# Two Fourier inputs as a ninth block group, three gate groups' first products moved to the conditioning stage, and a norm by token halves

## The chip, the cores and the metric

The kernel runs on one core of a Trainium2 chip. The metric is the device time of one execution in microseconds. Before the change three runs gave 1305.84, 1305.91 and 1307.22 us, with a median of 1305.91. A further execution was recorded by the hardware profiler, and every line of profile in this document is read from such a recording. The engines are called PE (the matrix engine, TensorE), ACT (ScalarE), DVE (VectorE), POOL (GpSimd) and SP (SyncE); all but DVE issue DMA transfers here.

## The reference

One layer of a backbone block on 512 tokens of width 2048 (`D`), with 256 context tokens; all data are float32. Cut to what matters here:

```python
shift, scale, gate = jnp.split(silu_c @ w_ada[l] + b_ada[l], 3, axis=-1)
h = _modulate(_rmsnorm(xs, norm_g[l]), shift[:, None], scale[:, None])   # xn * (1 + scale) + shift
...
p = h @ w_l                                   # 2048 -> 9216 columns: q, k, v, z_a, u_b, z_b, g_a, g_b
attn = _attention(q, concat([k, kc]), concat([v, vc]))
...
g_a, g_b = jax.nn.sigmoid(p[..., GA]), jax.nn.sigmoid(p[..., GB])
y_a = (attn * jax.nn.silu(z_a)) @ w_pa
y_b = (_fourier_mix(u_b) * jax.nn.silu(z_b)) @ w_pb   # real part of a 2-D FFT over 512 tokens x 128 channels, 4 channel groups
y = (g_a * y_a + g_b * y_b) @ w_o
new_xs = xs + gate[:, None] * y               # then a last rmsnorm
```

## The kernel before

Every product of float32 values is made of three matmuls in a reduced format (`mm3`, L326): each operand is split into a high part (`split_from`, ACT at L177) and a low part (DVE at L178), and high times high, high times low and low times high are added in PSUM. So "a product" of a 128 x 128 block with 512 columns is three matmuls of the form 128x512. Weights arrive by DMA as pieces of 128 x 1024 values, 512 KB each, which a list of requests (`stream`, `get`) loads ahead and splits in turn.

The work runs in stages, one after another on PE.

**Conditioning stage** (L453 to L657). x is loaded transposed in chunks (`XCH`, L106, L465). `token_norms` (L480) squares it on ACT and DVE, sums over the width with eight float32 matmuls (L497), takes roots (L501) and a reciprocal (L502), and `spread` (L505) lays the result over all partitions. Then comes a loop over the 16 blocks `kb` of 128 features. `modulation(kb)` (L584) is a matvec of silu(c) with 2 MB of modulation weights, sixteen 32x256 matmuls (L534) on weights that lie in four buffers of 1 MB (`wada_load`, L460, by POOL's queue from kb 3 on). `columns` (L539) copies its result out (ACT, L542), turns it by two transposes (L545) and adds up four rows (DVE, L551), which gives shift and gain of this kb. Two PSUM buffers (`bank2`) take turns in it. `make_h` (L519) scales x (DVE, L521), and makes the high half (ACT, L522) and the low half (DVE, L523) of h. For kb from 8 on, `form_row` (L601) makes two of the sums of blocks that the groups need later. Between these, PE multiplies by columns that need only the h made so far: `start_work` (L559) computes u and z of the Fourier branch, 8 column tiles of 128 x 16 kb x 3 matmuls, in the order of `STEPS`. Here the weights are the stationary operand and the 512 tokens the moving one, so the sums lie channel by token. Half of them stay in PSUM; the others are added up in SBUF by DVE (L564).

**Fourier stage** (L661 to L728). `channels` multiplies u by a cosine and sine table over the 128 channels, `positions` by a table over the tokens, each time with 256 moving columns, 144 matmuls in all. `gate_b` multiplies by silu(z). The result goes to DRAM (`b_d`) and comes back during attention.

**Eight groups** of 1024 columns of the input projection (`KINDS`, L65): three with q and z_a, two with g_a, one with k and v, two with g_b. A group is a product of h (512 x 2048) by 2048 x 1024 weights cut into 2 x 2 blocks, computed with seven block products instead of eight (Strassen's method in Winograd's form). `PRODUCTS` (L55) names for each product the form of h, what weights it takes, and its accumulator; P1, Q5, P2, Q6, P7, Q3 and Q4 run in the order `ONE_GROUP` (L57). One block product is 8 blocks of k x 2 tiles of 128 tokens x 3 matmuls = 48 matmuls 128x512. Accumulator "a" lies in the PSUM tile x, "b" in y and "c" in x again. When a product ends, ACT or DVE takes the sum out (`steps`, L862 to L902): P1's is copied to `self.X` and Q5's to `self.Y`, by ACT; the others are combined by DVE and handed to `done`, which for a gate group applies a sigmoid and stores the result (`gate_done`). P2 goes on adding to P1's accumulator. Combined weights are made in four buffers `R` by DMAs that add (L281, POOL's queue); P2, P7 and Q3 take plain loads.

**After that** follow attention, with products of the other branch filled in between (`filler`, which first reads `b_d`), two groups for the branch projections (10, 11) and two for the output projection. The output group 8 runs in the order `OUT_GROUP` (L58), in which P1 and P2 stand side by side.

Most orders come from the program's text and from due times: `issue_after` puts an instruction behind another, a list of small jobs is called once per piece, and each engine executes its instructions in the order in which they stand. PE, ACT and DVE therefore wait in line: what stands behind a waiting instruction waits too.

## Time and profile before

| | before |
|---|---|
| median of three runs | 1305.91 us |
| profiled execution, its own time | 1305.55 us |
| span in the profile | 1303.3 us |
| PE, DVE, ACT busy | 1279.5, 995.1, 685.4 us |
| first product of the conditioning stage | 23.47 us |
| Fourier matmuls | 148.75 to 169.39 us |
| eight groups | 169.39 to 808.0 us |
| moved by DMA | 318.54 MB, mean 244 GB/s |

The span runs from the first to the last recorded instruction; the execution's own time has 2.25 us around it. Busy times are sums over instructions. PE's matmuls overlap, so the duration of a single one is longer than the distance to the next. A group shows as one line and operation with "out<-in" by the tiles' names (buffer numbers left out), and in brackets behind a row stands the engine's idle time just before it and whose result ended it. DMA share is the busy share of 16 DMA engines.

### The profile page before, as it was taken

The numbers are of one execution on the slowest core, as the hardware profiler recorded it, in microseconds if no ns is written. First come the engines' busy times: TensorE is split into PE (matmuls) and PEld (weight loads), VectorE is DVE, ScalarE is ACT, GpSimd is POOL, SyncE is SP. The second block draws the span as 40 slices with busy tenths as digits, with TensorE's granted clock in tenths as the row PEclk, the third lists the DMA queues.
The fourth block names the chain that finished last, engine by engine and source line by source line (L and its number), as shares of the span: only waits on it lengthen the run. The fifth ranks groups of instructions, "written<-read, shape, count | busy, mean of one in ns | idle before, by whom it ended". The sixth has DMA issues, their size and how long they took to land.

```text
span 1303.3 us, 17544 instructions
## 1 busy us (share of the span) xinstructions
PE 1279.5 (98%) x6522; PEld 1047.4 (80%) x6522; DVE 995.1 (76%) x1295; ACT 685.4 (53%) x1079; POOL 180.6 (14%) x244
## 2 busy tenths in 40 slices
PE   6999999999999999999999999999999999999997
PEld 3577888888888888888888888888888888888885
DVE  4666899979688887657687766688798867887676
ACT  5222655555556465444254554666666646464544
POOL 0110011110202111011021010011110212221210
PEclk9999999999999999999999999999999999999999
DMA  9898487887899988976879897468872899998985
GB/s 382 338 373 349 178 244 183 242 243 255 209 284 260 265 287 271 292 209 179 273 200 267 294 224 258 169 221 245 251 230 82 236 246 250 244 212 232 220 205 173
DMA packets 103718, 318.54 MB, mean 244 GB/s; under 512 B 9808, under 2 KB 33104, under 8 KB 99280
## 3 DMA queue, kind: packets, MB, share of 16 engines
q0 software_dynamic: 30288, 123.75, 40.4%
q1 hardware_dynamic: 48720, 163.65, 35.3%
q10 hardware_dynamic: 24624, 30.02, 6.6%
q8 instruction: 51, 0.84, 0.2%
q14 instruction: 35, 0.29, 0.1%
HBM read 283.30 MB, written 34.09 MB: 244 GB/s over the span
## 4 chain that ended last, share of the span: by engine, by line
PE 91%; DMA 3%; DVE 2%; ACT 2%; issue 1%; SPq 0%; ACTq 0%; DVEq 0%
PE banks L328 10%; PE banks L329 10%; PE banks L330 10%; PE x L328 9%; PE x L330 9%; PE x L329 9%; PE y L329 7%; PE y L328 7%; PE y L330 7%; PE pd L534 2%; PE banks L1294 2%; PE pb L328 2%; PE pb L330 2%; PE pb L329 2%; DMA wa<-in_w_ss 1%; PE pc L328 1%
## 5 line engine op out<-in xcount | busy, mean ns | idle before, releaser
L177 ACT ACTIVATE whi<-R 128x1024 fp32r<-128x1024 f32 x138 | 145.2, 1059 | 140.2 <-PE banks L330 47.3
L178 DVE TENSOR_TENSOR wlo<-R,whi 128x1024 fp32r<-128x1024 f32 x138 | 167.5, 1221 | 55.4 <-ACT whi L177 55.2
L178 DVE TENSOR_TENSOR wlo<-wr,whi 128x1024 fp32r<-128x1024 f32 (+1 forms) x123 | 148.5, 1212 | 63.4 <-ACT whi L177 63.2
L177 ACT ACTIVATE whi<-wr 128x1024 fp32r<-128x1024 f32 (+1 forms) x123 | 128.8, 1051 | 116.6 <-PE y L330 37.4
L328 PE MATMUL banks<-whi,s 128*128 128x512 f32 x396 | 157.1, 397 | 2.2 <-DVE ev L862 1.5
L330 PE MATMUL banks<-whi,s 128*128 128x512 f32 x396 | 155.2, 392 | 0.0
L329 PE MATMUL banks<-wlo,s 128*128 128x512 f32 x396 | 155.1, 392 | 0.0
L328 PE MATMUL x<-whi,s 128*128 128x512 f32 x352 | 137.2, 390 | 0.0
L330 PE MATMUL x<-whi,s 128*128 128x512 f32 x352 | 137.0, 389 | 0.0
L329 PE MATMUL x<-wlo,s 128*128 128x512 f32 x352 | 137.0, 389 | 0.0
L328 PE MATMUL y<-whi,s 128*128 128x512 f32 x316 | 123.1, 389 | 0.4 <-DVE cxe L1015 0.4
L329 PE MATMUL y<-wlo,s 128*128 128x512 f32 x316 | 123.1, 390 | 0.3 <-DVE wlo L178 0.3
L330 PE MATMUL y<-whi,s 128*128 128x512 f32 x316 | 122.8, 389 | 0.0
L281 POOL DMA_DIRECT2D R<-in_w_g x64 | 55.9, 874 | 420.2 <-DVE wlo L178 247.5
L177 ACT ACTIVATE s<-wr 128x512 fp32r<-128x512 f32 (+2 forms) x93 | 60.4, 676 | 68.6 <-DMA wr<-cf_d 21.8
L178 DVE TENSOR_TENSOR s<-wr,s 128x512 fp32r<-128x512 f32 (+2 forms) x93 | 66.8, 749 | 31.7 <-ACT s L177 30.9
L328 PEld LDWEIGHTS banks<-whi,s 128*128 128x128 f32 x396 | 74.4, 188 | 17.7 <-ACT whi L177 1.9
L330 PEld LDWEIGHTS banks<-whi,s 128*128 128x128 f32 x396 | 74.4, 188 | 15.5
L329 PEld LDWEIGHTS banks<-wlo,s 128*128 128x128 f32 x396 | 74.4, 188 | 14.0 <-DVE wlo L178 0.2
L330 PEld LDWEIGHTS x<-whi,s 128*128 128x128 f32 x352 | 66.1, 188 | 13.8
L329 PEld LDWEIGHTS x<-wlo,s 128*128 128x128 f32 x352 | 66.1, 188 | 13.6
L328 PEld LDWEIGHTS x<-whi,s 128*128 128x128 f32 x352 | 66.1, 188 | 13.6
(293 smaller groups left out, 2829.4 us busy)
## 6 DMA issues: line engine op xcount, KB each, us to landing
wr<-in_w_g SPq DMA_DIRECT2D x128, 512.0 KB, 5.2
R<-in_w_g POOLq DMA_DIRECT2D x64, 512.0 KB, 7.5
wa<-in_w_ss POOLq DMA_DIRECT2D x26, 1024.0 KB, 8.2
R<-in_w_g SPq DMA_DIRECT2D x32, 512.0 KB, 5.6
wr<-in_w_gate SPq DMA_DIRECT2D x32, 512.0 KB, 5.1
wr<-in_w_o SPq DMA_DIRECT2D x24, 512.0 KB, 7.7
R<-in_w_o POOLq DMA_DIRECT2D x24, 512.0 KB, 9.5
wr<-in_w_pab SPq DMA_DIRECT2D x20, 512.0 KB, 6.4
```

The lines of the kernel that those rows point to most:

```text
L177: first = nc.scalar.activation(hi, src, ACT.Copy)
L178: return first, nc.vector.tensor_tensor(lo, src, hi.bitcast(F32), op=ALU.subtract)
L281: nc.gpsimd.dma_start(chain[e.pc], e.nxt, accum_op=ALU.add)
L328: nc.tensor.matmul(o, ah, bh, start=start, stop=False, skip_group_check=cont)
L329: nc.tensor.matmul(o, ah, bl, start=False, stop=False, skip_group_check=cont)
L330: nc.tensor.matmul(o, al, bh, start=False, stop=stop, skip_group_check=cont)
L534: last = nc.tensor.matmul(acc[32 * j : 32 * j + 32, :256], c2[:, 8 * h + k, :], w[:, k, :], start=n < 4, stop=n >= KK - 4)
L1294: nc.tensor.transpose(tp[:, k * P : (k + 1) * P], p[:, k * P : (k + 1) * P], ident)
```

## The change

1. u and z become a ninth group of 1024 columns (`U`, kind "uz"), the first in `ORDER`, with the seven block products in the order `OUT_GROUP`. Their sums are stored to DRAM (`uz_d`). The forms of h that group 0 made during its products (`between`) are made in U.
2. The conditioning stage multiplies instead by the first 512 columns of groups 3, 6 and 7 (`EARLY`), all 16 blocks of k: 3 x 2 token tiles x 16 x 3 = 288 matmuls, which are P1 and P2 of these groups. h is now the stationary operand. The three sums stay in PSUM (`sums_e`). The sum over the first 8 blocks is P1: after kb 7 it is copied and stored (`x1_kept`, `x1_d`). After kb 15 the whole sum gets its sigmoid and is stored (`gate_kept`). Groups 3, 6 and 7 then run five products (`EARLY_GROUP`, `early_end`) and load P1's sum as `X`.
3. x lies as [half of tokens, feature block, 256]. Only the first 256 tokens are normed at the start (`norm_first`), and `make_h` works on them alone for kb below 8. The second half is loaded on POOL's queue (`X_MORE`), squared in kb 6 and 7, normed after kb 7 (`norm_second`), and used from kb 8 on; `form_row` scales the second half of the earlier blocks.
4. The matvecs and norms use two halves of one PSUM tile (`two_d`) in turn.
5. The Fourier stage goes behind the last group. u's sums and differences, and the splits of the tables, are jobs in the last group; `positions` comes first (48 matmuls 128x512), then `channels` (24 matmuls 128x512, and 16 transposes of z). Nothing goes through `b_d`.
6. The pieces of context work spread over 20 pieces of group 3 and 28 of group 4.

```diff
+U = -1
+EARLY = (3, 6, 7)
+EARLY_PIECES = ([((0, 0),), ((0, 1), (0, 2)), ((1, 0), (1, 1)), ((1, 2),)]
+                + [p for k in range(2, KK, 2) for p in (((k, 0), (k, 1)), ((k, 2), (k + 1, 2)), ((k + 1, 0), (k + 1, 1)))])
+EARLY_GROUP = ("Q3", "Q5", "Q6", "P7", "Q4")
+ORDER = (U, *range(len(KINDS)))
+X_MORE = {3: (0,), 4: (4,), 5: (8,), 6: (12,)}
+def products_of(g):
+    return EARLY_GROUP if g in EARLY else OUT_GROUP if g == U else ONE_GROUP
...
+    sums_e = [psp.tile([P, 2, 512], F32, tag=t, bufs=n, name=uid("pb")) for t, n in (("x", 2), ("x", 2), ("y0", 1))]
+    two_d = psp.tile([P, 2, 512], F32, tag="y1", bufs=1, name="pd")
+    def bank2():
+        turn_d[0] ^= 1
+        return two_d[:, turn_d[0], :]
+    def load_x(h, a, n, q=None):
+        (q or nc.sync).dma_start(xt[:, h, a : a + n, :], xT[h, :, a : a + n, :])
     for a, n in XCH:
-        nc.sync.dma_start(xt[:, a : a + n, :], xT[:, a : a + n, :])
+        load_x(0, a, n)
...
+    def square_more(i):
+        if i % 4 == 0:
+            squares.append(new_ev())
+        t = squares[-1][:, 0, :]
+        q = 2 * i
+        a, b = (t[:, :256], t[:, 256:]) if i % 4 == 0 else (squares[-1][:, 1, :256], squares[-1][:, 1, 256:])
+        for o, k in ((a, q), (b, q + 1)):
+            nc.scalar.activation(o, xt[:, 1, k, :], ACT.Square)
+        if i % 4:
+            nc.vector.tensor_tensor(t, t, squares[-1][:, 1, :], op=ALU.add)
+    def norm_second():
+        acc = bank2()
+        n = 0
+        for s in squares:
+            for k in range(2):
+                nc.tensor.matmul(acc[:, :256], ones, s[:, 0, 256 * k : 256 * k + 256], start=n == 0, stop=n == 3)
+                n += 1
+        norm_root(1, acc[:, :256])
+        nc.scalar.copy(rx[:, 1, :], spread(1, acc[:, 256:]))
...
+    def normed(kb, hs, rr):
+        v = xt[:, hs, kb, :]
+        return nc.vector.scalar_tensor_tensor(v, v, gain[:, kb, 0:1], rr, op0=ALU.mult, op1=ALU.mult)
+    def x1_kept(i, a):
+        t = new_ev()
+        nc.scalar.copy(t, a)
+        nc.scalar.dma_start(x1_d[i], t.rearrange("p t c -> p (t c)"))
+    def early_work():
+        for n, (_, what) in enumerate(early_pieces()):
+            wh, wl = get(("early", n))
+            for m, (kb, i) in enumerate(what):
+                a = sums_e[i]
+                for t in range(2):
+                    c = slice(P * t, P * t + P)
+                    mm3(a[:, t, :], hhi[kb][:, c], hlo[kb][:, c], wh[:, m, :], wl[:, m, :], kb == 0, kb in (7, KK - 1),
+                        cont=kb >= 8)
+                if kb == 7:
+                    x1_kept(i, a)
+                elif kb == KK - 1:
+                    gate_kept(EARLY[i], 0, 0, a, None)
+                yield kb
...
+        if kb in X_MORE:
+            for a in X_MORE[kb]:
+                load_x(1, a, 4, nc.gpsimd)
+        if kb in (6, 7):
+            for i in range(4 * (kb - 6), 4 * (kb - 6) + 4):
+                square_more(i)
+        if kb == 7:
+            norm_second()
...
+        def early_end(self, name, a):
+            if name == "Q3":
+                self.V = self.new()
+                nc.scalar.copy(self.V, a)
+            elif name == "Q5":
+                self.Y = self.new()
+                nc.scalar.copy(self.Y, a)
+            elif name == "Q6":
+                sub(self.X, a, self.X)
+                sub(self.V, self.X, self.V)
+                sub(self.Y, self.X, self.Y)
+                self.done(0, 1, self.X, self.X)
+            elif name == "P7":
+                sub(self.V, self.V, a)
+                self.done(1, 1, self.V, self.V)
+            elif name == "Q4":
...
+    def fourier():
+        def positions(g):
+            acc, c = pair("x"), slice(P * g, P * g + P)
+            for e in range(2):
+                for r in range(2):
+                    mm3(acc[:, e, :], uf[e][0][:, r, c], uf[e][1][:, r, c], fs[e][0][:, r, :], fs[e][1][:, r, :],
+                        r == 0, r == 1)
+                split_from(acc[:, e, :].rearrange("p (c n) -> p c n", c=2), hi[:, :, e, :], lo[:, :, e, :])
+        def channels(g):
...
+                nc.tensor.transpose(zt[:, t * P : t * P + P], z[t // 2][:, k : k + P], ident)
...
+                mm3(acc, fc[0][:, 0, s], fc[0][:, 1, s], hi[:, c, :], lo[:, c, :], c == 0, c == 1)
...
+        positions(0)
+        positions(1)
+        channels(0)
+        positions(2)
+        channels(1)
+        positions(3)
+        channels(2)
+        channels(3)
...
-    for g, kind in enumerate(KINDS):
+    for g in ORDER:
+        kind = "uz" if g == U else KINDS[g]
+        if g in EARLY:
+            group.X = new_ev()
+            nc.gpsimd.dma_start(flat(group.X), x1_d[EARLY.index(g)])
+            elif (g, name) == (LAST, "Q6"):
+                jobs += [lambda: None, u_forms]
+    fourier()
```

## The prediction

> **What bounds the kernel now.** I read the page first: the busy shares, the slices, the chain that ended last; then PE's waits, then windows cut where the stages change.

> ```profile
> span 1303.3 us, 17544 instructions
> PE 1279.5 (98%) x6522; PEld 1047.4 (80%) x6522; DVE 995.1 (76%) x1295; ACT 685.4 (53%) x1079; POOL 180.6 (14%) x244
> PE   6999999999999999999999999999999999999997
> PE 91%; DMA 3%; DVE 2%; ACT 2%; issue 1%; SPq 0%; ACTq 0%; DVEq 0%
> ...
> PE pd L497 <- DVE s L496: 8.5, 1, 8.5
> PE banks L328 <- DVE ev L862: 1.5, 1, 1.5
> ...
> 0.00:24.00 24.00, 13.85 (x66) 7.01 (x67) 12.17 (x28) 15.52 (x27) 1.90 (x11) 1.00 0.93 370
> 24.00:42.00 18.00, 17.53 (x117) 9.98 (x115) 7.76 (x16) 4.35 (x9) 2.34 (x4) 1.00 1.01 417
> 42.00:148.75 106.75, 106.61 (x766) 74.75 (x765) 73.42 (x143) 35.86 (x53) 11.83 (x22) 1.00 0.82 313
> 148.75:169.39 20.64, 20.38 (x158) 19.57 (x156) 20.04 (x29) 11.29 (x19) 0.54 (x1) 1.00 0.61 226
> 169.39:245.90 76.51, 76.51 (x340) 63.37 (x339) 73.68 (x86) 43.36 (x64) 9.97 (x12) 1.00 0.82 223
> 655.00:731.50 76.50, 76.50 (x339) 63.38 (x338) 56.73 (x64) 38.01 (x67) 12.29 (x13) 1.00 0.87 261
> 731.50:808.00 76.50, 76.50 (x341) 63.34 (x340) 50.97 (x54) 38.28 (x46) 9.67 (x14) 1.00 0.82 229
> ```

> TensorE bounds it: 1279.5 of 1303.3 us busy, so all its idle time is 23.8 us, 8.5 of it one wait at the start. Seven columns follow each window: length, then busy time of PE, PEld, DVE, ACT and POOL, granted clock, DMA share, GB/s. From 42 us on PE is full. The first two windows show what else is near its limit: 417 GB/s at a DMA share of 1.01. A group of seven products is 76.50 us, all PE; in the first one DVE is busy 73.68 of it. With PE that full, the change can win only the PE work it removes, and loses every us in which its new order leaves PE waiting.

> **Prices.** Three timelines of PE, its neighbours beside it (start, duration, engine, line):

> ```profile
> 88.55 1.93 PE L534 MATMUL pd<-wa,c 128*32 128x256 f32 x32
> 90.42 0.50 PE L328 MATMUL pc<-s,whi 128*128 128x512 f32 x1
> 90.61 0.37 ACT L542 COPY ado<-pd 128x256 f32<-128x256 f32 x1 [5.81 <-PE pd L534]
> 91.22 0.38 PE L545 MATMUL pd<-ident,ado 128*128 128x128 f32 x2
> 91.36 0.47 PE L328 MATMUL pc<-s,whi 128*128 128x512 f32 x1
> 91.71 0.17 DVE L551 TENSOR_REDUCE adr<-pd 128x4 f32<-128x16 f32 x1 [2.36 <-PE pd L545]
> 92.38 0.75 DVE L521 SCALAR_TENSOR_TENSOR xt<-xt,gain,rx 128x512 f32<-128x512 f32 x1
> 93.16 0.72 ACT L522 ACTIVATE s<-xt,shift 128x512 fp32r<-128x512 f32 x1 [2.18 <-DVE xt L521]
> 93.29 0.40 PE L330 MATMUL pc<-s,wlo 128*128 128x512 f32 x1
> 93.62 1.93 PE L534 MATMUL pd<-wa,c 128*32 128x256 f32 x32
> 93.64 0.47 DVE L608 SCALAR_TENSOR_TENSOR Z<-xt,d 128x256 f32<-128x256 f32 x1
> ...
> 147.62 0.39 PE L329 MATMUL pc<-s,whi 128*128 128x512 f32 x1
> 147.84 0.39 PE L330 MATMUL pc<-s,wlo 128*128 128x512 f32 x1
> ...
> 160.03 0.28 PE L328 MATMUL pb<-fsq,ah 128*128 128x256 f32 x1
> 160.15 0.28 PE L329 MATMUL pb<-fsq,ah 128*128 128x256 f32 x1
> ```

> Dense matmuls start 0.2275 us apart at 512 columns (147.62, 147.84) and 0.12 at 256 (160.03, 160.15), less than the shown durations, since they overlap. The kb chain is: matvec ends about 90.42, its columns turn from 91.22 (0.80 later), and the high half of h is there at 93.16 + 0.72 = 93.88: 3.46 us after the matvec. At 256 columns xt costs about 0.47 (L608) for 0.75, and hi about 0.37 (the 256-wide copy) for 0.72: 2.83.

> **The PE work itself.** Removed: 384 products of u and z (128x512) and the 144 Fourier matmuls at 256. Added: 3 groups x 16 k x 2 columns x 3 = 288 in the conditioning stage; nine groups with 6 x 336 + 3 x 240 = 2736 instead of 8 x 336 = 2688; the late Fourier with 48 + 24 and 16 transposes. In 512-wide matmuls +24, in 256-wide -144: 5.5 - 17.3 + 2 for the transposes = -10 us. If PE stayed dense that would be the result. It does not, for the reasons below.

> **Start of the conditioning stage.** The first early product waits for the first norm, now on 256 columns, yet the built program puts the four second-half x loads on POOL's queue without a wait, ahead of the modulation weights of kb 3, so both halves share the saturated engines (1.01) from the start. I take 22 us. The trace of before starts its first product at:

> ```profile
> 23.47 0.73 PE L328 MATMUL pb<-s,whi 128*128 128x512 f32 x2 [0.30 <-ACT s L522]
> ```

> [...]

> **A pair of kb.** In the built program's PE order, a pair below kb 8 reads: 18 products of kb, 7 matvec matmuls, transposes, 9 of the next matvec, 12 products, 7 matvecs, 3 products, transposes, 3 products, 9 matvecs, 18 products. Before, nine products of older k stood behind the transposes (91.36 to 93.29); now products that need this very kb's hi stand there. Between the matvec's end and them lie, in the even case, the transposes (0.2) and nine of sixteen matvec matmuls (9/16 of the 1.87 from 88.55 to 90.42: 1.05); in the odd case six products (1.4) more. Against the 2.83, PE idles about 1.6 us and 0.2 us, with the crossings to the next engine and the split of the weights in ACT's queue 1.7 and 0.65. A pair is 36 x 0.2275 + 2 x 1.87 + 0.4 = 12.3 us of work, with 2.35 of waits 14.65. DMA is close below: a pair loads 4.19 MB of modulation and 1.57 MB of early weights, 13.9 us at the 417 GB/s above. For kb from 8, hi is 512 wide again (3.46) and DVE norms the second half besides: 15.4 us. Also, matvecs now all use one two-part PSUM tile, so each waits for the reduce of the kb before it; that keeps them from running ahead.

> **The second norm.** kb 7's products run from 22 + 3.5 x 14.65 = 73 to 77.5 us. Behind them in PE's order stand half of the norm matmuls, the spread and matvec(8); in ACT's order, the x1 copies (the last waits for these products) stand ahead of eight squares. Chain, from rows of the first norm in before:

> ```profile
> L501 ACT ACTIVATE s<-pd,eps_t 32x128 f32<-32x128 f32 x4 | 1.4, 359 | 2.2 <-PE pd L497 2.2
> L502 DVE RECIPROCAL s<-s 128x128 f32<-128x128 f32 x1 | 1.0, 953 | 3.0 <-ACT s L501 3.0
> L865 ACT COPY ev<-x 128x1024 f32<-128x1024 f32 x8 | 8.1, 1012 | 6.7 <-PE x L330 6.7
> ```

> Copy 1.4 with its start, eight 256-wide squares 3.2, add and matmuls 2, roots 1.5, reciprocal 0.6, spread and copy 1.5, matvec 1.1, the chain of kb 8 3.5, and about 0.3 for each of ten crossings between engines: 17.7 us, with some 6 us of matmuls in it. So PE idles 11 us (5 if the squares come early, 14 if reciprocals don't shrink). First product of kb 8 at 95, kb 15's at 95 + 3.5 x 15.4 = 149, early work over at 153 to 154; I take 154 against 169.4, where the groups began: **-15.4** (bounds: 131, the floor of 52 MB at 417 GB/s plus the last chain, to 162).

> **Groups.** 48 more matmuls of 0.2275: **+10.9**. U's first weights: ACT has the last sigmoids and DMA issues ahead of their split, **+1.4** (0 to 3). Then the neighbours: in before, a (tile x) and b (y) alternate, so an eviction runs under the next product. Now two products on one accumulator stand side by side: P1, P2 and Q5, Q6 in U; Q3, Q5 and Q5, Q6 in each early group; and P7's reader, a DVE subtraction, stands ahead of Q4. The program makes the first matmul of the second wait for the copy. The one such place in before is an output group:

> ```profile
> 1150.03 0.39 PE L330 MATMUL banks<-whi,s 128*128 128x512 f32 x1
> 1150.27 1.03 PE L1408 MATMUL banks<-ident,s 128*128 128x128 f32 x8
> 1151.53 0.50 PE L328 MATMUL banks<-whi,s 128*128 128x512 f32 x1 [0.23 <-ACT s L865]
> 1150.46 1.01 ACT L865 COPY s<-banks 128x1024 f32<-128x1024 f32 x1 [0.57 <-PE banks L330]
> ```

> 1151.53 - 1150.03 is 1.50 from start to start instead of 0.2275: 1.27 us, filled there by transposes. Of eleven such places, I count eight with nothing between: **+10.2** (five at 6.4; eleven at 14, DVE's longer if it is behind).

> **Weights in the early groups.** They drop two products of seven, but of their loads only P2's four pieces (2.1 MB, 5 us at 417 GB/s); x1 comes on top (0.5 MB), and the last group also gets tables, u and z (3.3 MB, 8 us). By share x length group 6 was 0.87 x 76.5 = 66.6 and group 7 62.7; now 62.8 and 67, into 2 x (54.6 + 3.8) = 116.8. The pieces ahead carry up to 10 of these 13 us: **+5** (0 to +15, more if accumulating loads clog).

> **Late Fourier.** 72 x 0.2275 = 16.4, 16 transposes about 1.8; and channels(0) and channels(3) wait for the splits of positions, some 2.5 with nothing else in PE's order: **+20.7** (18.2 to 24). Its cover in before, the leftover u and z products, is gone.

> **Sum.** -15.4 + 1.4 + 10.9 + 10.2 + 5 + 20.7 = +32.8 on the profiled execution's 1305.55 us: 1338.4. That execution lies 0.36 below the median of the runs shown, 1305.91, so 1338.7; I say **1338**.

> **Rivals.** *Stages hide their stalls, faster:* the conditioning runs at the DMA floor (over at 131), second squares and roots run early, and every copy is covered. Then -38.4 + 10.9 + 18.2 = -9.3: 1297. It decides at an early end near 138 with copies free. For it speaks the DMA share near 1; against it, PE's order leaves no older product to run. Chance 0.06. *Pairs as forecast, no norm gap:* 22 + 7.5 x 14.65 + 4 = 136, so -33.4 in place of -15.4: 1321. Chance 0.13; ACT's order speaks against it. *The late weights bind:* groups 6 and 7, and 3 before them, run at their loads, +20 in place of +5: 1354. Chance 0.13. *Nothing to see* (gains and losses cancel): 0.03.

> [...] Chance 0.05 that it shows.

> **Numbers.** The forecast as summed has 0.60. The range, 1316 to 1356, takes in the norm gap's absence and the late weights; what is left out is the faster case and sums of all bad bounds. A measurement tells 0.2% (2.6 us) from no change: faster 0.06, same 0.03, slower 0.91.

> **What would show it.** U's first products on x near 155 us instead of 169.39; PE's waits at the early products for ACT's hi, up to 2 us each; one hole of about 10 us near 80 to 95; waits at Q5, Q6 and Q4 of groups 3, 6, 7 for copies, over 1 us each; a Fourier stretch of 20 us between the last group and attention. It is wrong if the early work ends before 140, if those copies leave no gap, or if PE's idle total stays under 35 us.

## The result, and the profile after

The changed kernel takes 1399.02 us (median of three runs, 1396.54 to 1399.72) against 1305.91 before: a ratio of 1.0705, with a 95% interval of 1.0681 to 1.0729. It is slower by 93 us, where the prediction said 32 and a range up to 1356. The profiled execution is one of 1399.02 us with a span of 1397.2, so 93.9 us of span are to be found. Its page:

```profile
span 1397.2 us, 17469 instructions
PE 1310.0 (94%) x6434; PEld 1053.8 (75%) x6434; DVE 1006.4 (72%) x1288; ACT 703.5 (50%) x1102; POOL 187.8 (13%) x257
PE   6978889999999989989998889999999999999997
PEclk9989999999999999999999899999999999999999
PE 67%; DMA 11%; issue 9%; DVE 7%; ACT 4%; POOL 1%; ACTq 0%; SPq 0%; DVEq 0%; POOLq 0%
```

PE's idle time rose from 23.8 to 87.2 us, and its busy time from 1279.5 to 1310.0 although it has less to do. In the chain that ended last PE fell from 91% to 67%, and DMA rose from 3% to 11%. PEclk, which was full throughout, has two slices below 9. PE's waits, in us in total, times, longest:

```profile
PE y L333 <- ACT ev L902: 10.4, 3, 7.0
PE pd L534 <- DVE s L533: 7.8, 4, 5.5
PE pd L558 <- DVE ev L550: 6.3, 1, 6.3
PE y L333 <- ACT ev L899: 5.6, 2, 4.5
PE pb L333 <- ACT s L628: 4.5, 5, 2.1
PE pd L591 <- ACT ado L588: 4.5, 9, 0.6
PE x L333 <- DVE ev L896: 3.6, 2, 3.3
```

L899 and L902 are the copies of Q3 and Q5 in the early groups, L896 the subtraction ahead of Q4, L550 and L533 the sums of squares of the two norms. So the places that the prediction named are there, but the sizes are not its own. Windows of the changed kernel, cut at its stages (columns as in the prediction):

```profile
0.00:29.00 29.00, 17.20 (x65) 9.60 (x65) 10.35 (x30) 15.23 (x35) 4.15 (x15) 1.00 0.93 360
29.00:89.90 60.90, 56.77 (x386) 36.17 (x386) 26.36 (x49) 19.58 (x29) 7.53 (x14) 1.00 0.96 375
89.90:110.40 20.50, 10.32 (x80) 5.59 (x79) 8.42 (x22) 6.55 (x17) 1.90 (x4) 0.67 0.47 167
110.40:171.20 60.80, 54.19 (x351) 35.38 (x351) 35.00 (x67) 22.17 (x29) 4.57 (x9) 0.97 0.80 311
171.20:256.10 84.90, 79.21 (x338) 62.51 (x338) 69.17 (x69) 43.05 (x43) 6.83 (x8) 1.00 0.89 272
256.10:485.80 229.70, 228.82 (x1010) 188.93 (x1009) 185.44 (x217) 120.65 (x212) 31.80 (x36) 1.00 0.85 242
485.80:549.80 64.00, 58.14 (x245) 47.13 (x244) 50.33 (x67) 33.37 (x58) 10.86 (x12) 0.95 0.90 249
549.80:635.50 85.70, 81.40 (x350) 66.34 (x349) 61.94 (x94) 42.72 (x59) 6.89 (x8) 0.98 0.86 273
750.40:821.90 71.50, 60.11 (x242) 48.28 (x243) 50.04 (x55) 30.75 (x55) 11.91 (x13) 0.90 0.90 265
821.90:883.72 61.82, 56.49 (x254) 46.16 (x253) 41.97 (x43) 30.55 (x37) 9.52 (x13) 1.00 0.82 220
883.72:906.44 22.72, 19.33 (x85) 14.40 (x84) 13.86 (x21) 9.57 (x17) 1.07 (x2) 1.00 0.31 106
906.44:1397.20 490.76, 476.01 (x2550) 401.19 (x2550) 379.01 (x475) 286.92 (x447) 79.70 (x110) 0.99 0.77 210
```

The rows are the start; kb 0 to 7; the gap of the second norm; kb 8 to 15; U; groups 0 to 2; group 3; group 4; group 6; group 7 (the group with k and v, between 4 and 6, is left out); the Fourier stage; attention and the rest. Groups 0 to 2 run as they did before. Group 3 takes 64.0 us and group 6 71.5 for 240 matmuls of 0.2275, which are 54.6.

One correction to the table of before: its eight groups end at 819.6 us, not at 808, which lies within the last product. PE's timeline and the last window of before:

```profile
819.62 0.39 PE L330 MATMUL x<-whi,s 128*128 128x512 f32 x1
821.48 0.47 PE L328 MATMUL banks<-whi,s 128*128 128x512 f32 x1 [1.47 <-DVE ev L862]
```

```profile
821.48:1303.30 481.82, 471.20 (x2550) 398.81 (x2550) 377.80 (x474) 286.06 (x446) 79.83 (x109) 0.99 0.79 214
```

With that, the 93.9 us by stage, beside the prediction's terms:

| stage | before | after | difference | forecast |
|---|---|---|---|---|
| to the first product of the groups | 169.4 | 171.2 | +1.8 | -14.0 |
| groups | 650.2 | 712.5 | +62.3 | +26.1 |
| Fourier stage up to attention's first matmul | 1.9 | 22.7 | +20.8 | +20.7 |
| attention to the end | 481.8 | 490.8 | +9.0 | 0 |

In the groups, 2904 matmuls (nine groups and the context's 168) at 0.2275 are 660.7 us, so 51.8 of the 712.5 are lost; before it was 650.2 - 649.7 = 0.5. By groups: U 8.5, groups 0 to 2 0.4, group 3 9.4, groups 4 and 5 together 9.5, group 6 16.9, group 7 7.2.

### The profile page after: what moved, and what is told of

It reads as the page before. It is cut to its first block, busy times and chain, and to the rows that moved or that the text cites. A ratio compares the mean times of both kernels' runs of the same rounds, so it can differ in the third digit from the quotient of the medians.

```text
span 1397.2 us, 17469 instructions
## 1 busy us (share of the span) xinstructions
PE 1310.0 (94%) x6434; PEld 1053.8 (75%) x6434; DVE 1006.4 (72%) x1288; ACT 703.5 (50%) x1102; POOL 187.8 (13%) x257
## 4 chain that ended last, share of the span: by engine, by line
PE 67%; DMA 11%; issue 9%; DVE 7%; ACT 4%; POOL 1%; ACTq 0%; SPq 0%; DVEq 0%; POOLq 0%
PE banks L333 10%; PE banks L334 9%; PE banks L335 9%; PE x L333 6%; PE x L334 5%; PE x L335 5%; PE y L333 5%; PE y L334 5%; PE y L335 5%; DMA R<-in_w_g 2%; DMA wr<-in_w_g 2%; DMA wa<-in_w_ss 2%; PE banks L1378 2%; DVE wlo L182 2%; PE pd L578 1%
## 5 line engine op out<-in xcount | busy, mean ns | idle before, releaser
L182 DVE TENSOR_TENSOR wlo<-wr,whi 128x1024 fp32r<-128x1024 f32 (+1 forms) x142 | 171.2, 1214 | 97.9 <-ACT whi L181 97.9
L181 ACT ACTIVATE whi<-wr 128x1024 fp32r<-128x1024 f32 (+1 forms) x142 | 148.0, 1051 | 149.4 <-PE y L335 49.4
L333 PE MATMUL y<-whi,s 128*128 128x512 f32 x356 | 141.8, 398 | 20.0 <-ACT ev L902 10.4
L333 PE MATMUL x<-whi,s 128*128 128x512 f32 x364 | 143.0, 393 | 4.3 <-ACT whi L181 3.2
L334 PE MATMUL x<-wlo,s 128*128 128x512 f32 x364 | 143.2, 394 | 2.5 <-DVE wlo L182 2.5
L334 PE MATMUL y<-wlo,s 128*128 128x512 f32 x356 | 141.1, 396 | 3.0 <-DVE wlo L182 2.9
L335 PE MATMUL x<-whi,s 128*128 128x512 f32 x364 | 142.2, 391 | 0.0
L335 PE MATMUL y<-whi,s 128*128 128x512 f32 x356 | 140.5, 395 | 0.0
L333 PEld LDWEIGHTS y<-whi,s 128*128 128x128 f32 x356 | 68.0, 191 | 37.5 <-ACT ev L902 11.7
L181 ACT ACTIVATE s<-wr 128x512 fp32r<-128x512 f32 (+3 forms) x81 | 54.4, 687 | 59.0 <-DMA wr<-cf_d 17.5
L333 PEld LDWEIGHTS x<-whi,s 128*128 128x128 f32 x364 | 68.8, 189 | 20.1 <-ACT whi L181 4.0
L334 PEld LDWEIGHTS y<-wlo,s 128*128 128x128 f32 x356 | 68.1, 191 | 18.9 <-DVE wlo L182 4.9
```

What stands on the lines that cost most here:

```text
L181: first = nc.scalar.activation(hi, src, ACT.Copy)
L182: return first, nc.vector.tensor_tensor(lo, src, hi.bitcast(F32), op=ALU.subtract)
L333: nc.tensor.matmul(o, ah, bh, start=start, stop=False, skip_group_check=cont)
L334: nc.tensor.matmul(o, ah, bl, start=False, stop=False, skip_group_check=cont)
L335: nc.tensor.matmul(o, al, bh, start=False, stop=stop, skip_group_check=cont)
```

## The experiments

All are edits of the changed kernel, compared with its 1399.0 us; each ratio is to the kernel before. A group's loss is its time less 0.2275 us for each of its matmuls. Two cautions for reading them. Runs of one kernel lie up to 10 us apart (the last experiment). And stages that an edit doesn't touch move as well: in the six profiles whose groups are those of the changed kernel, these take 712.5 to 720.0 us, group 3 loses 7.5 to 12.9 and group 6 16.6 to 19.3; in all thirteen profiles attention to the end takes 484.7 to 490.8. A total alone therefore decides little between theories that lie a few us apart.

**Q3 between Q5 and Q6, same accumulator.** The sums of the three are taken out in the new order.

```diff
-EARLY_GROUP = ("Q3", "Q5", "Q6", "P7", "Q4")
+EARLY_GROUP = ("Q5", "Q3", "Q6", "P7", "Q4")
...
-                sub(self.Y, self.X, self.Y)
+                nc.vector.tensor_tensor(self.Y, self.V, self.Y, op=ALU.add)
+                self.V, self.Y = self.Y, self.V
```

> Early groups in the order Q5, Q3, Q6, P7, Q4, all three of Q5, Q3, Q6 still on the accumulator in y. Theory A (the adding loads): Q6's weights are made by a DMA that adds to what Q5 has just split, so with no product in between they land too late; with Q3 between, the waits in y of groups 3, 6 and 7 fall from some 26 us to the bare copies, about 7 us: 1380 us, 15 to 20 less than the changed kernel's 1399. Theory B (copies of 1.27 us only, as predicted): nothing changes in kind, 1399. Theory C (the DMA engines are full in these groups): 1397 to 1399.

Measured: 1406.2 us, ratio 1.0762 [1.0731, 1.0794]; slower. Theory A held in group 6 alone, where the wait of 6.97 us became 1.10 and the group's loss 8.2 us. In group 3 it was worse: the copy of Q5 now came 14.84 us late, and the group lost 19.3. Rows of ACT there, with one issue of SP and PE's next product:

```profile
489.34 0.35 SPq L217 DMA_DIRECT2D wr<-in_ctx_toks  x1
490.17 1.04 ACT L181 ACTIVATE whi<-wr 128x1024 fp32r<-128x1024 f32 x1
496.17 0.63 ACT L181 ACTIVATE s<-wr 128x512 fp32r<-128x512 f32 x1 [4.95 <-DMA wr<-in_w_g]
503.06 1.06 ACT L1070 ACTIVATE wr<-wr 128x1024 f32<-128x1024 f32 x1 [6.26 <-DMA wr<-in_ctx_toks]
...
510.47 0.99 ACT L902 COPY ev<-y 128x1024 f32<-128x1024 f32 x1
511.51 0.80 PE L333 MATMUL y<-whi,s 128*128 128x512 f32 x1 [14.84 <-ACT ev L902]
```

ACT's queue holds the next product's splits, and the squares of a piece of context tokens that was asked for at 489.34 and came at 503, ahead of the copy (L902); behind these stand some 6 us of splits and of squares for the last q group's norm, ahead of the copy too. The sum in y had been ready since 496.7. The copy takes 0.99 us; what is late is what stands ahead of it.

**Q3 in a PSUM tile of its own.** As the one before, with Q3's sum in x, so that it needs no copy and Q5's copy has Q3 to run under.

```diff
+EARLY_GROUP = ("Q5", "Q3", "Q6", "P7", "Q4")
...
-            if name == "Q3" and self.g >= BRANCH_A:
+            if name == "Q3" and (self.g >= BRANCH_A or self.g in EARLY):
                 which = "d"
...
+                sub(self.V, a, self.X)
+                sub(self.Y, self.V, self.Y)
+                nc.vector.tensor_tensor(self.X, self.V, self.acc["d"], op=ALU.add)
```

> As the one before, and Q3 in a PSUM tile of its own in x, so that neither Q3 nor Q6 waits for a copy; only P7 to Q4 stay neighbours. Theory A: the waits of the three groups nearly vanish, 1371 to 1377 us, 22 to 28 less than 1399, and some 6 less than the other order alone. Theory B: six copies of 1.27 us gone, 1391. Theory C: 1396 to 1399.

Measured: 1390.6 us, 1.0643 [1.0599, 1.0687]: B's number, but not by B's sum. No wait for a copy is left in the early groups. Group 6 loses 8.3 us for 16.9, and group 7 1.5 for 7.2. Yet group 3 loses 13.6, since it still waits 4.16 us, now for ACT's split itself, and the first product of group 6 in y waits 4.74 us for the context's last subtraction. In the profiled execution (1392.9 us) all groups together take 710.3 us, only 2.2 less than in the changed kernel; the rest of its gain stands in stages that were not touched. So the order helps groups 6 and 7; in group 3, with the copies gone, the waits that stood ahead of them on ACT remain; and that the total met B's is luck.

**The adding loads left out.**

```diff
-        if e.nxt is not None:
+        if e.nxt is not None and e.key[1] not in EARLY:
             nc.gpsimd.dma_start(chain[e.pc], e.nxt, accum_op=ALU.add)
```

> In groups 3, 6 and 7 the DMAs that add to R are left out, so that Q6 and Q4 take weights that were not combined. Theory A and C alike blame these 24 transfers, A by their latency between Q5 and Q6, C by their share of the DMA engines: the waits in these three groups fall from some 36 us to the copies of 7 to 10, 1372 to 1378 us. Theory D (the eviction copies and ACT's and DVE's queues are the limit without them): 1390 or more.

In groups 3, 6 and 7 the weights of Q6 and Q4 then stay uncombined, and what it computes is not the layer.

Measured: 1383.7 us, 1.0586 [1.0547, 1.0625], between the two. Its waits for the two copies:

```profile
PE y L333 <- ACT ev L899: 6.9, 3, 5.2
PE y L333 <- ACT ev L902: 3.3, 3, 1.1
```

The copy of Q5 (L902) now costs 1.1 us in each of the three groups: its longest wait, 6.97 in group 6, was made by the adding loads, and that group loses 7.3 us for 16.9. Whether by their place between Q5 and Q6 or by their share of the DMA engines, this run alone can't say; that the first experiment, which keeps all loads and only puts Q3 between, takes the same wait to 1.10 speaks for the place. The copy of Q3 in group 3 (L899) still waits 5.2 us: there it was not. In the changed kernel, the place in group 6 reads:

```profile
768.83 0.86 POOL L285 DMA_DIRECT2D R<-in_w_g  x1 [2.64 <-DVE wlo L182]
775.92 1.15 ACT L181 ACTIVATE s<-R 128x512 fp32r<-128x512 f32 x2 [3.46 <-DMA R<-in_w_g]
778.72 1.15 ACT L181 ACTIVATE s<-R 128x512 fp32r<-128x512 f32 x2 [1.65 <-DMA R<-in_w_g]
779.77 0.99 ACT L902 COPY ev<-y 128x1024 f32<-128x1024 f32 x1
780.82 0.80 PE L333 MATMUL y<-whi,s 128*128 128x512 f32 x1 [6.97 <-ACT ev L902]
```

The last adding load is issued when DVE has split Q5's piece in the same R (768.83), its piece is split at 778.72, and only then ACT reaches the copy of a sum that was ready at 773.85. In the order of the full groups P2, a product of plain loads, lies in between and covers this.

**Groups 4, 6 and 7 early.**

```diff
-EARLY = (3, 6, 7)
+EARLY = (4, 6, 7)
...
-    n = 20 * (g - NQZ) + 4 * products_of(g).index(name) + pc
+    n = 28 * (g - NQZ) + 4 * products_of(g).index(name) + pc
```

> Groups 4, 6 and 7 instead of 3, 6 and 7 have their first two products in the conditioning stage; the context work lies on 28 pieces of group 3 and on group 4, as before the change. Theory C (the DMA engines are full where an early group's six loads in 55 us meet the context's loads, in group 3): groups 3 and 4 lose under 6 us together instead of some 16, the loss at the entry to the group with k and v is gone, 1387 to 1391 us. Theory A (an early group loses by its own order, wherever it stands): 9 us go from group 3 to group 4, 1397 to 1400.

Measured: 1388.1 us, 1.0620 [1.0580, 1.0660], as theory C had it, though not in all parts, and 3.4 us of the gain stand ahead of U (167.7 us for 171.2), where nothing was changed. Early group 4 waits 1.10 us at each of its two copies and loses 2.7 us in its first three products, where group 3 lost 9.0; group 3, now a full group with the context work, loses 0.2. The 6.7 us lost in group 4's last product are gone too; but in its P7 5.9 us go, where a low half waits in DVE's queue (2.51 us) and Q4 waits for the last subtraction (1.52). Group 3's loss thus comes from the early order at this place. What it meets there is of two kinds: the four pieces of context tokens, and the norm of the last q group, whose squares (L971) ACT still has to do; early group 4, behind a gate group, has neither. In the changed kernel, the sum that the first copy takes is ready at 496.80 us, and ACT comes to it at 500.28, after eight such squares, one of which waits for DVE:

```profile
496.82 0.28 ACT L971 ACTIVATE y<-ev 128x128 f32<-128x128 f32 x1 [1.50 <-DVE y L975]
500.28 0.99 ACT L899 COPY ev<-y 128x1024 f32<-128x1024 f32 x1
```

A piece of context tokens holds ACT up for 1.37 us ahead of that. Which of the two makes the loss was not tried by itself.

**Context rows earlier.**

```diff
-    if n % 7 == 4 and 18 <= n < 46:
-        return "cr", n // 7 - 2
+    if n % 4 == 2 and 18 <= n < 34:
+        return "cr", n // 4 - 4
```

> The four context rows at pieces 18, 22, 26, 30 of groups 3 and 4 instead of 18, 25, 32, 39. Theory A (their stored rows come back too late for the group with k and v, and ACT waits for them ahead of group 4's last splits): the 6.7 us lost near 615 to 635 us go, 1392 us. Theory B (the loads of group 4's last product are late by themselves): 0 to 2 us, 1397 to 1399.

Measured: 1393.0 us, 1.0662 [1.0601, 1.0722], runs of 1389.7 and 1396.2. The stretch that was to lose nothing still lost 5.9 us for 6.7 (1.2 in group 4's Q3 and 4.7 in its Q4), so theory A falls, whatever the time; the cause of this loss stays open.

**U in the order of the other groups.**

```diff
-    return EARLY_GROUP if g in EARLY else OUT_GROUP if g == U else ONE_GROUP
+    return EARLY_GROUP if g in EARLY else ONE_GROUP
```

The forms of h that are made during U's products follow the new order.

> U in the order P1, Q5, P2, Q6, P7, Q3, Q4 of the other full groups. Theory A (neighbours on one accumulator cost 1.1 us each in U, the rest of its 8.5 us is a late first split): U's loss falls by 2 to 3 us, 1395 to 1397 us. Theory B (U loses because nothing was loaded and split ahead of it, and Q5's adding loads come at once): U loses as much as now or more, 1399 to 1402.

Measured: 1402.1 us, 1.0726 [1.0687, 1.0766]; theory B. The loss moved to U's first product, where PE waited 8.73 us for DVE's first low halves. The other six products then lose nothing. U starts with one piece split ahead, and loses 8.3 us in the one order and 12.0 in the other.

**The whole norm at the start.** Both halves of x are loaded and normed first; h below kb 8 still has 256 columns.

```diff
     for a, n in XCH:
-        load_x(0, a, n)
+        for h in range(2):
+            load_x(h, a, n)
...
-        if kb in (6, 7):
-            for i in range(4 * (kb - 6), 4 * (kb - 6) + 4):
-                square_more(i)
-        if kb == 7:
-            norm_second()
```

The norm's own lines are widened to 512 tokens.

> The norm of all 512 tokens at the start as before the change, nothing of it after kb 7; h still made for 256 columns below kb 8. Theory A (the gap of 20 us around the second norm, idle and then at half clock, lies on the path): U's first products come 12 to 18 us earlier than 171.2, at 153 to 159; 1381 to 1387 us. Theory B (the weights' DMA sets the pace of this stage, and makes up for a gap): U starts at 167 to 171, 1395 to 1399. Beside it: with 512-wide norm matmuls PE is warm earlier, matvec rows at 1.07 us for 1.94.

Measured: 1386.4 us, 1.0611 [1.0579, 1.0644]; theory A. U starts at 158.5 for 171.2, 12.7 us earlier, and the gain stays to the end. From the first product, at 28.28, to U it takes 130.2 us for 142.2. The matvec rows came at 1.07 us, as was expected beside it.

**The second norm earlier.**

```diff
-        if kb in (6, 7):
-            for i in range(4 * (kb - 6), 4 * (kb - 6) + 4):
+        if kb in (3, 4, 5, 6):
+            for i in range(2 * (kb - 3), 2 * (kb - 3) + 2):
                 square_more(i)
-        if kb == 7:
+        if kb == 6:
             norm_second()
```

> The second half's norm moved forward: squares in kb 3 to 6, the rest of it after kb 6's h. Theory A (the gap comes from where it stands, behind the copies of kb 7 and eight squares in a row): the idle stretch of 20 us shrinks to under 5, U at 158 to 162 for 171.2, 1386 to 1390 us, like the whole norm. Theory H (two norms instead of one cost the stage wherever they stand): 1394 or more.

Measured: 1387.1 us, 1.0614 [1.0591, 1.0636]; theory A again, U at 161.4. Its first product came late (30.73 us); from there to U it takes 130.7 us for 142.2. In the stretch that now holds the second norm PE is busy 9.57 of 10 us:

```profile
78.80:88.80 10.00, 9.57 (x72) 6.89 (x73) 7.99 (x18) 4.37 (x9) 1.07 (x2) 1.00 0.66 228
```

So not the second norm costs these 11 us, but its place behind kb 7's copies.

**The gap filled with small matmuls.**

```diff
+                with tc.issue_after(last_early[0].ins):
+                    for _ in range(24):
+                        nc.tensor.matmul(spare, ones, ones, start=True, stop=True)
...
+        with tc.issue_after(last_early[0].ins):
+            for _ in range(8):
+                nc.tensor.matmul(spare, ones, ones, start=True, stop=True)
```

> 24 small matmuls on ones behind kb 7's last product and 8 more behind the second norm's last matmul, into a spare half of the PSUM tile, so that PE is busy through the idle 6.35 and 1.94 us of the gap. Theory E (the idle gap drops PE to half rate, and the matmuls behind it pay for that): the half-clock stretch of 13.65 us from 93.9 shrinks to 3.4 or to nothing, from kb 7's last product to kb 8's first are 17 to 18 us for 20.5, U starts 2.5 to 3.5 us earlier; 1395 to 1397 us. Theory I (ACT's and DVE's chain sets the gap's length): half clock or not, 20 us or more, 1398 to 1400.

Measured: 1397.0 us (four runs, 1396.3 to 1399.9), 1.0698 [1.0677, 1.0719], too little to tell. U starts at 168.6, 2.6 us earlier, but 1.6 of these are there already at the first product (27.40), which the edit doesn't touch. The half-clock stretch shrank from 13.65 to 6.8 us, but from kb 7's last product to kb 8's first it still took 21 us (from 87.1 to 108.4): theory I. The gap's length is set by ACT's and DVE's chain; PE's own matmuls at the end of it, still at half rate here (3.64 us for the matvec at 100.70, as in the changed kernel for that at 102.70), were not made faster.

**Matmuls ahead of and between the first norm's.**

```diff
+        for _ in range(6):
+            nc.tensor.matmul(wacc[:, :P], ones, ones, start=True, stop=True)
...
             nc.tensor.matmul(acc, ones, a, start=q == 0, stop=q == KK - 2)
+            for _ in range(3):
+                nc.tensor.matmul(wacc[:, :P], ones, ones, start=True, stop=True)
```

> Small matmuls on a tile of ones, to a sum that nobody reads, ahead of and between the first norm's matmuls. Theory E (PE runs at half its rate until it has been busy for a while, and the half-wide norm matmuls with their gaps leave it so until 32 us): the first matvec rows last 1.07 us for 1.94, first product at 24 to 26 us for 28.99, U 4 to 5 us earlier, 1394 to 1395 us. Theory F (x and the first modulation weights set the start): first product at 28 to 29 us, 1398 to 1399.

Measured: 1405.5 us, 1.0752 [1.0701, 1.0803]. The matvec rows came down to 1.07 us, as E has it, but the first product stands at 28.46 us for 28.99, where F has it. This doesn't decide, for two reasons. A chunk of x landed later in this execution (ACT waits 3.65 us for it, in the changed kernel 1.78; with U in the other order, where the start is untouched, it is 4.13), so that the first matvec stands at 19.22 for 17.53; and the three matmuls behind the spread ran slow again (2.81 us at 24.54, in the changed kernel 2.87, in the kernel before 1.46). What the half rate costs is read below, from other profiles. Why the groups of this kernel, which were not touched, took 7 us more is not settled.

**The three matmuls without use left out.**

```diff
-            warm(3, o)
```

> The three matmuls on ado between the norm's spread and the first product, whose sum nobody reads, are left out. They write the PSUM tile that also holds the spread norm, and at half rate they last 2.87 us. Theory G (DVE's first scaling of x waits for them, since the tile is one): first product at 25.8 to 26.5 us for 28.99, U 2.5 to 3 us earlier, 1396 us. Theory F (x and the first weights set the start): first product within 1 us of 28.99, 1398 to 1399.

Measured: 1396.5 us, 1.0685 [1.0655, 1.0716], runs of 1393.4 and 1399.6. The first product stands at 27.05 us, 1.9 earlier and short of G's window, though x came late here as well (first matvec at 19.38 for 17.53): from there to the first product it takes 7.67 us for 11.46. U stands at 170.6, 0.5 earlier. In the changed kernel the wait is plain:

```profile
25.00 2.87 PE L603 MATMUL pb<-ado,ones 128*128 128x256 f32 x6
27.91 0.48 DVE L621 SCALAR_TENSOR_TENSOR xt<-xt,gain,pb 128x256 f32<-128x256 f32 x1 [3.07 <-PE pb L603]
28.99 0.79 PE L333 MATMUL pb<-whi,s 128*128 128x512 f32 x1 [1.11 <-ACT s L628]
```

So the wait is as G says. Of the 3.8 us that the way got shorter, 1.0 is a wait for the second load of weights that the late start hid, so taking the matmuls away is worth some 2.8 us there, and nothing sure at the end.

**Together.** The whole norm, no matmuls without use, Q3 apart, groups 4, 6 and 7.

> Whole norm, no matmuls without use at the start, Q3 in a tile of its own, groups 4, 6 and 7 early. If the losses are the separate ones found (13, 3, 8 and 11 us, with some of them overlapping), 1364 to 1370 us. The rest of the distance to 1306 then stands in the late Fourier stage (20), in 48 more matmuls (11), in U's late splits (8), in the waits of the last two groups and the start of attention. Rival: the weights' loads set the pace and take back what is gained, over 1378.

Measured: 1369.6 us (four runs, 1364.7 to 1374.7), 1.0467 [1.0445, 1.0489], in the window. U starts at 158.5, attention at 883.3 (906.4 in the changed kernel). The profiled execution is the slowest of the four: U starts 12.7 us earlier in it, and the groups take 702.0 us for 712.5, less of a gain than the two edits of the groups promised, since early group 4 loses 12.2 us here. So that the sum lands in the window is in part luck. 63 us to the kernel before are left; no version tried here beats it.

## Why the prediction was wrong

Its direction was right and its size was not; the sum of +32.8 should have been +93.9.

- *Start, "I take 22 us"*: 28.99. Wrong by 7. The second x half on POOL's queue had been seen; what was not counted lies between the first matvec and the first product, which stand 11.46 us apart (17.53 to 28.99), and in the kernel before 6.38 (17.09 to 23.47). The matmuls there take twice as long (a matvec half 1.94 us for 1.07); DVE's first scaling waits 3.07 us for three matmuls in the tile of the spread norm; and matvec(0) itself waits for the roots (1.35 us, "pd L578 <- ACT root L514"), since norms and matvecs now share one PSUM tile. Other profiles tell the first two apart. Without the three matmuls the way was some 2.8 us shorter. In the kernel with the gap filled, whose start has the same code, the transposes took 0.41 us for 0.66 and the first product's first matmul 0.50 for 0.79, while the changed kernel's matmuls stand 0.43 us apart until 32.14; from the transposes to the first product it took 3.71 us for 6.04. The changed kernel's transposes, then this kernel's transposes and first product:

```profile
22.95 0.66 PE L591 MATMUL pd<-ident,ado 128*128 128x128 f32 x2 [0.58 <-ACT ado L588]
```

```profile
23.69 0.41 PE L599 MATMUL pd<-ident,ado 128*128 128x128 f32 x2 [0.58 <-ACT ado L596]
27.40 0.50 PE L333 MATMUL pb<-whi,s 128*128 128x512 f32 x1 [1.11 <-ACT s L636]
```

  So the half rate costs the start at least 2.3 us. The two overlap, as the three matmuls are long because of the half rate (2.87 us, in the kernel before 1.46).
- *A pair of kb, 14.65 us*: 15.33 (transposes at 60.85 and 76.18). Nearly right, by the wrong terms. The waits for hi, put at 2.35 us, are 0.82 (0.48 for ado and 0.34 for the reduce); instead the matvecs, put at 1.87, cost 2.5, because each is now cut in two by products. In rows:

```profile
61.62 1.48 PE L578 MATMUL pd<-wa,c 128*32 128x256 f32 x18 [0.34 <-DVE adr L597]
63.14 0.50 PE L333 MATMUL pb<-whi,s 128*128 128x512 f32 x1
66.12 1.06 PE L578 MATMUL pd<-wa,c 128*32 128x256 f32 x14
67.12 0.50 PE L333 MATMUL pb<-whi,s 128*128 128x512 f32 x1
```

  Nine of the sixteen matmuls (each counts twice in the rows) take 1.52 us to the next product and seven 1.00. All of kb 0 to 7 took 60.9 us, where the forecast from 22 to 77.5 is 55.5.
- *The second norm's gap, 17.7 us*: 20.5, its mechanism right: PE idles 10.2 us of it, where 11 were forecast, but its matmuls take 10.3 for 6. Two experiments show its cause, the place of the second norm behind kb 7's copies on ACT; moved or removed it gives 10 to 13 us back. With it the conditioning ends at 171.2 for 155.4.
- *Copies of 1.27 us, eight of them, +10.2*: the price is right where nothing else is late (1.10 us in rows, in U twice and in early group 4 twice). What failed is the assumption that the copy starts when its sum is ready. ACT's queue is in order, and other work stands ahead of the copy; where that is late, the copy waits with it: 6.97 us in group 6, behind the split of a piece from an adding load, and 4.52 in group 3, behind squares and splits.
- *Weights in the early groups, +5, "the pieces ahead carry up to 10 of these 13 us"*: this is the step that failed most. With the copies, 15.2 us were forecast for the groups beside their matmuls, and 51.8 were lost. The prediction set the loads of whole groups against the DMA's rate and let the pieces ahead cover most of the rest. What the runs showed instead is no smooth overload but two places: Q6's adding loads, with no plain product between Q5 and Q6 (the wait goes from 6.97 to 1.10 us in group 6 when they are left out or Q3 is put between, and the group's loss from 16.9 to 7 or 8), and the early order right behind the last q group and among the context's loads (9.0 us in group 3, 2.7 with the early group elsewhere; which of the two it is stays open). In U, where 1.4 us were put for the first split, PE idles 5.7: 2.2 for two copies and 3.5 for late low halves. The rest stays open: 6.7 us in group 4's last product, in group 6 3.3 for the subtraction ahead of Q4, and in group 7 2.9 for a load of q. The rival that named late weights had the right sign, and a price of 20 that was too small.
- *Late Fourier, +20.7*: +20.8. Right.
- *Attention, nothing*: +9.0, not in the sum at all; in the twelve edited kernels, whose attention is the same, it is 2.9 to 8.0. Its first stretch lost some 3.5 us: pab's weights are asked for only at 902.2 us, and land at 910.6. A stretch near 1007 lost 1.4 and one near 1100 4, of which no experiment was made.
- *The half clock, with a chance of 0.05 and no term in the sum*: it showed. The changed kernel's profile has eight stretches of it within PE's work, each behind a step of 3.413 us in which PE was idle for 1.55 to 3.41 (last section). The mean granted clock is 0.981 there, 0.969 to 0.987 in the executions of the twelve edits, and 0.998 in the profile of before. That before reads 1.00 up to its last matmul is no sign against it: after the one wait of 8.5 us at the start none of that kernel's waits is longer than 1.5. Windows at four of the drops, and two rows inside one:

```profile
93.90:107.50 13.60, 8.36 (x46) 4.64 (x46) 4.95 (x11) 2.78 (x9) 1.07 (x2) 0.50 0.18 56
500.10:506.90 6.80, 5.58 (x13) 4.42 (x14) 6.80 (x9) 2.28 (x4) 3.10 (x3) 0.50 1.05 275
776.60:786.80 10.20, 5.98 (x14) 4.73 (x15) 7.15 (x8) 3.88 (x6) 3.10 (x4) 0.50 0.77 191
810.70:814.10 3.40, 3.40 (x9) 2.63 (x8) 1.49 (x2) 1.22 (x2) 0.00 (x0) 0.50 1.02 401
```

```profile
783.12 0.63 PE L335 MATMUL y<-whi,s 128*128 128x512 f32 x1
783.55 0.63 PE L333 MATMUL y<-whi,s 128*128 128x512 f32 x1
```

  At a granted clock of 0.50 matmuls stand 0.43 us apart for 0.2275. Eight such stretches hold 36.8 us of PE's busy time, 28.4 of them outside the norm's gap; 28.4 x (1 - 0.2275 / 0.43) makes some 13 us that the waits cost once more. It is worked out, not shown by taking it away: in the gap itself, where it was tried, filling gave nothing sure.

## What to carry to other kernels

When a product is followed by one on the same accumulator, don't price the eviction by its own duration (0.99 us in group 6), but by what stands ahead of it in its engine's queue, and by when that will have its data (PE waited 6.97 us there). A DMA that adds to a buffer is a chain: split, issue, landing, split (issued at 768.83 us and split at 778.72 there); keep a piece of work without such a load between two links (with Q3 between, that wait was 1.10). In a kernel whose PE is full, moving work into a stage with little slack costs the wait and, by the estimate above, the lower clock after it (some 13 us here), so look for the new waits before counting the matmuls saved. And before a total is taken for the proof of a theory, see in the trace that the time went where the theory has it.

## What the runs showed of the hardware

The profile's clock column has a blind side: before the first record it reads 1.00, yet the matvec rows at 17.5 us last 1.94 us for 1.07, so PE ran at half rate until the first record at 32.4 us. In the kernel before, whose 512-wide norm matmuls kept PE busy from 8.5 to 17.1 us, that record stands at 11.6 us.
